# Loading a kernel's first batch in long runs: rotary embedding and scores on one core

## The chip, the cores and the metric

The kernel runs on one core of one Trainium2 chip. The metric is the device time of one execution in microseconds (us). The same kernel varies by some 0.2% from run to run.

## The reference

```python
batch, seq, heads, dim = 16, 512, 16, 64          # q, k: [batch, seq, heads, dim], float32
q_rot = np.concatenate([q1 * cos_q - q2 * sin_q, q1 * sin_q + q2 * cos_q], axis=-1)
k_rot = np.concatenate([k1 * cos_q - k2 * sin_q, k1 * sin_q + k2 * cos_q], axis=-1)
scores = np.einsum('bshd,bthd->bsht', q_rot, k_rot)   # [16, 512, 16, 512], float32
```

67 MB are read and 268 MB are written, against little arithmetic.

## The kernel before

A partition holds four neighbouring positions of a batch, the "slots" `c = 0..3`. A batch of q or of k is then 16 KB of unbroken memory per partition. VectorE rotates, TensorE transposes and multiplies, ScalarE copies the scores to a stage buffer of 4 MB, and SyncE asks for all large transfers on one queue. There are three stage buffers; the third holds the first batch of q and k at the start.

The first batch is treated apart: its unit of work is not a slot but a group of four heads over all four slots, so that the compute can start when these heads have landed. Its loads follow that grouping:

```python
    def load_units(which, head, heads):                 # runs of heads*64*4 bytes
        ...
        src = dram[which][0, :, :, head : head + heads, :]
        nc.sync.dma_start(t.rearrange("p c (h d) -> p c h d", d=D), src)
        for h in range(0, heads, G):
            units[which, (head + h) // G] = t[:, :, D * h : D * (h + G)]
...
        for head, heads in ((0, G), (G, H - G)):        # G = 4: 1 KB runs, then 3 KB runs
            load_units("k", head, heads)
            load_units("q", head, heads)
        load("k", 1)
        load("q", 1)
...
        for which in ("k", "q"):
            run(rope(which, 0))                          # rotate heads 0..3 of all four slots
            tr_act(which, 0)
        for i in range(C):                               # first batch; its stores are 1 MB each
            ...
            for p in range(HP):
                scores(i, p, st)
                ...
                if p == 3 and i < 2:
                    load("kq"[i], 2)                     # third batch of k, of q
        load("k", 3)
        for i in range(C, NST):                          # steady part; a 4 MB store each
            ...
```

## Time and profile before

| | before |
|---|---|
| median of 3 runs | 799.22 us (799.08 to 800.84) |
| span of the profiled run | 798.6 us |
| bytes moved | 336.17 MB |
| busy: PE, DVE, ACT | 690, 545, 561 us |
| share of q1 in the 16 DMA engines' span | 98.7% |

A busy TensorE at 86% might look like the bound; but the DMA engines are busy all the time, so only their idle time and the length of their packets count. The lines are shown in the prediction.

### The profile page before, as it was taken

The page shows a single profiled execution, that of the slowest core. Times are in us where ns is not written, and L with a number is a line of the kernel's source. Part 1 is how long each engine was busy: PE and PEld are TensorE (multiplying, and loading weights), DVE is VectorE, ACT ScalarE, POOL GpSimd, SP SyncE. Part 2 cuts the span into 40 slices and gives each one's busy share as a digit, 9 for nine tenths or more (in the row PEclk, how much of TensorE's full clock was granted, in tenths as well). Part 3 has the DMA queues.
Part 4 walks back from the last instruction along what each step waited for, and adds up shares of the span by engine and source line. Part 5 has one row for each costly group of instructions (what it writes and reads, how often), then busy time and mean ns, then how long its engine had stood idle before and what let it go on. Part 6 is the DMA issues. An engine that isn't in the chain of part 4 may idle for free.

```text
span 798.6 us, 7719 instructions
## 1 busy us (share of the span) xinstructions
PE 690.1 (86%) x3072; PEld 299.2 (37%) x3072; DVE 544.5 (68%) x516; ACT 561.3 (70%) x647; POOL 0.7 (0%) x6
## 2 busy tenths in 40 slices
PE   4999998997979789797897988979889798899970
PEld 2444443433434334343343433424334243344420
DVE  7999987676857568575685766857758577586300
ACT  3888886776848668485785866858668586688770
POOL 0000000000000000000000000000000000000000
PEclk9999999899989899898998998999989899899995
DMA  9999999999999999999999999999999999999995
GB/s 357 421 411 435 437 423 433 423 427 440 421 431 429 429 437 427 436 421 434 426 432 434 431 420 429 434 429 437 427 424 407 443 422 440 423 404 419 426 426 235
DMA packets 17988, 336.17 MB, mean 421 GB/s; under 512 B 1824, under 2 KB 3104, under 8 KB 4384
## 3 DMA queue, kind: packets, MB, share of 16 engines
q1 hardware_dynamic: 17664, 335.55, 98.7%
q8 instruction: 24, 0.39, 0.2%
q10 hardware_dynamic: 288, 0.13, 0.1%
q14 instruction: 12, 0.10, 0.0%
HBM read 67.24 MB, written 268.44 MB: 420 GB/s over the span
## 4 chain that ended last, share of the span: by engine, by line
DMA 51%; PE 38%; ACT 4%; DVE 3%; issue 1%; ACTq 0%; SPq 0%
DMA out_dram<-st 48%; PE ps L166 29%; PE bank L127 9%; ACT st L173 4%; DMA q_sb<-in_q_dram 2%; DVE part L106 1%; DMA sin_t<-in_sin_dram 0%; DVE q_sb L107 0%; DVE k_sb L111 0%; DVE k_sb L107 0%; DVE q_sb L111 0%; DVE early L107 0%; DVE kT_t L142 0%; ACTq L281 0%; DVE early L111 0%
## 5 line engine op out<-in xcount | busy, mean ns | idle before, releaser
L173 ACT COPY st<-ps 128x1024 f32<-128x1024 f32 x512 | 495.0, 1019 | 203.4 <-DMA out_dram<-st 112.3
L166 PE MATMUL ps<-kT_t,qT_t 64*128 64x512 f32 x2048 | 547.9, 653 | 72.1 <-ACT st L173 72.1
L166 PEld LDWEIGHTS ps<-kT_t,qT_t 64*128 64x128 f32 x2048 | 185.0, 197 | 261.9 <-issue 140.6
L142 DVE COPY qT_t<-bank 128x512 f32<-128x512 f32 x118 | 81.5, 691 | 203.8 <-PE bank L127 203.8
L127 PEld LDWEIGHTS bank<-ident,q_sb 128*128 128x128 f32 x480 | 55.5, 151 | 102.4 <-issue 99.8
L127 PE MATMUL bank<-ident,q_sb 128*128 128x128 f32 x480 | 86.7, 308 | 0.9 <-PE ps L166 0.9
L127 PEld LDWEIGHTS bank<-ident,k_sb 128*128 128x128 f32 x480 | 50.5, 141 | 95.0 <-DVE k_sb L107 37.5
L127 PE MATMUL bank<-ident,k_sb 128*128 128x128 f32 x480 | 78.7, 287 | 1.2 <-DVE qT_t L142 1.2
L142 ACT COPY kT_t<-bank 128x512 f32<-128x512 f32 x122 | 72.5, 599 | 6.2 <-PE bank L127 6.2
L107 DVE TENSOR_TENSOR q_sb<-q_sb,cos_t 128x1024 f32<-128x1024 f32 x60 | 73.5, 1225 | 2.1
L111 DVE TENSOR_TENSOR k_sb<-k_sb,part 128x1024 f32<-128x1024 f32 x60 | 73.5, 1225 | 2.1
L107 DVE TENSOR_TENSOR k_sb<-k_sb,cos_t 128x1024 f32<-128x1024 f32 x60 | 73.5, 1225 | 2.0
L106 DVE TENSOR_TENSOR part<-q_sb,ss_t 128x1024 f32<-128x1024 f32 x60 | 73.5, 1225 | 2.0
L106 DVE TENSOR_TENSOR part<-k_sb,ss_t 128x1024 f32<-128x1024 f32 x60 | 73.0, 1216 | 0.1
L111 DVE TENSOR_TENSOR q_sb<-q_sb,part 128x1024 f32<-128x1024 f32 x60 | 72.9, 1216 | 0.0
L127 PE MATMUL bank<-ident,early 128*128 128x128 f32 x64 | 10.5, 316 | 12.3 <-DVE early L111 10.4
L127 PEld LDWEIGHTS bank<-ident,early 128*128 128x128 f32 x64 | 8.3, 161 | 17.3 <-issue 13.2
L106 DVE TENSOR_TENSOR part<-early,ss_t 128x1024 f32<-128x1024 f32 x8 | 9.8, 1223 | 5.7 <-ACT ss_t L198 5.5
L111 DVE TENSOR_TENSOR early<-early,part 128x512 f32<-128x512 f32 x16 | 10.3, 687 | 0.2
L107 DVE TENSOR_TENSOR early<-early,cos_t 128x1024 f32<-128x1024 f32 x8 | 9.8, 1225 | 0.3
L142 ACT COPY qT_t<-bank 128x512 f32<-128x512 f32 x10 | 5.7, 630 | 3.2 <-PE bank L127 3.2
L142 DVE COPY kT_t<-bank 128x512 f32<-128x512 f32 x6 | 4.1, 684 | 0.0
(9 smaller groups left out, 2.8 us busy)
## 6 DMA issues: line engine op xcount, KB each, us to landing
out_dram<-st SPq DMA_DIRECT2D x58, 4096.0 KB, 24.1
k_sb<-in_k_dram SPq DMA_DIRECT2D x15, 2048.0 KB, 27.6
q_sb<-in_q_dram SPq DMA_DIRECT2D x15, 2048.0 KB, 27.6
out_dram<-st SPq DMA_DIRECT2D x16, 1024.0 KB, 13.7
out_dram<-st SPq DMA_DIRECT2D x1, 3584.0 KB, 22.8
out_dram<-st SPq DMA_DIRECT2D x1, 3328.0 KB
early<-in_k_dram SPq DMA_DIRECT2D x1, 1536.0 KB, 8.8
early<-in_q_dram SPq DMA_DIRECT2D x1, 1536.0 KB, 12.0
```

What stands on the lines that cost most here:

```text
L106: nc.vector.tensor_tensor(pv, xs, ss, op=mult)
L107: nc.vector.tensor_tensor(xc, xc, cs, op=mult)
L111: nc.vector.tensor_tensor(y, y, z, op=add)
L127: nc.tensor.transpose(bank[:, x, :], src, ident)
L142: copy(out=dst, in_=src)
L166: nc.tensor.matmul(out=po, lhsT=lhs[64 * r : 64 * r + 64, :], rhs=rh, start=True, stop=True)
L173: nc.scalar.copy(out=so, in_=si)
```

## The change

It means to make the first 4 MB faster (long runs in place of 1 KB and 3 KB ones) and to keep the queue filled until the first store by asking for the third k early.

```diff
-    def load_units(which, head, heads):
-        ...
+    first = {}
+    for x, which in enumerate("kq"):
+        t = early[:, C * H * D * x : C * H * D * (x + 1)]
+        first[which] = t.rearrange("p (c e) -> p c e", c=C)
+    units = {(w, n): first[w][:, :, G * D * n : G * D * (n + 1)] for w in "kq" for n in range(C)}
 ...
     def load(which, b):
 ...
+        for x, y in ((0, 1), (1, 2), (2, C)) if (which, b) == ("k", 0) else ((0, C),):
+            nc.sync.dma_start(
+                t[:, x:y].rearrange("p c (h d) -> p c h d", h=H), dram[which][b][:, x:y]
+            )
 ...
-        for t, src in ((cos_t, cos), (sin_t, sin)):
+        for t, src in ((sin_t, sin), (cos_t, cos)):
 ...
-        for head, heads in ((0, G), (G, H - G)):
-            load_units("k", head, heads)
-            load_units("q", head, heads)
-        load("k", 1)
-        load("q", 1)
+        for which, b in (("k", 0), ("q", 0), ("k", 1), ("q", 1), ("k", 2)):
+            load(which, b)
 ...
-                if p == 3 and i < 2:
-                    load("kq"[i], 2)
+                if p == 3 and i == 1:
+                    load("q", 2)
```

The unit of compute stays a group of heads over all slots. It now needs all pieces of a batch.

More of the change, by code (lines that the diff above doesn't have):

```diff
@@ L58 @@
     early = stage_pool.tile([P, 2 * C * H * D], fp32, tag="stage", name="early")
-    units = {}
-    used = [0]
-    def load_units(which, head, heads):
-        n = C * heads * D
-        t = early[:, used[0] : used[0] + n].rearrange("p (c e) -> p c e", c=C)
-        used[0] += n
-        src = dram[which][0, :, :, head : head + heads, :]
-        nc.sync.dma_start(t.rearrange("p c (h d) -> p c h d", d=D), src)
-        for h in range(0, heads, G):
-            units[which, (head + h) // G] = t[:, :, D * h : D * (h + G)]
+    first = {}
[3 more added lines that the diff above has]
+    units = {(w, n): first[w][:, :, G * D * n : G * D * (n + 1)] for w in "kq" for n in range(C)}
     batches = {}
@@ L76, in load @@
             return
-        t = in_pool.tile([P, C, H * D], fp32, tag=which + "_in", name=which + "_sb")
-        batches[which, b] = t
-        nc.sync.dma_start(t.rearrange("p c (h d) -> p c h d", h=H), dram[which][b])
+        if b == 0:
+            t = first[which]
+        else:
+            t = in_pool.tile([P, C, H * D], fp32, tag=which + "_in", name=which + "_sb")
+            batches[which, b] = t
+        for x, y in ((0, 1), (1, 2), (2, C)) if (which, b) == ("k", 0) else ((0, C),):
+            nc.sync.dma_start(
+                t[:, x:y].rearrange("p c (h d) -> p c h d", h=H), dram[which][b][:, x:y]
+            )
     def rope(which, n):
```

## The prediction

> **What bounds the kernel now.** I read the page's head and slices first, then its DMA queues, then the stretches of the start and of the end, then SyncE's issues in order of time, and last VectorE's first instructions.
>
> ```profile
> span 798.6 us, 7719 instructions
> ...
> DVE  7999987676857568575685766857758577586300
> ...
> DMA  9999999999999999999999999999999999999995
> GB/s 357 421 411 435 437 423 433 423 427 440 421 431 429 429 437 427 436 421 434 426 432 434 431 420 429 434 429 437 427 424 407 443 422 440 423 404 419 426 426 235
> ...
> q1 hardware_dynamic: 17664, 335.55, 98.7%
> ```
>
> The DMA row is full in 39 of 40 slices, and SyncE's queue q1 alone fills 98.7% of the 16 engines' span. So the kernel takes what 336 MB take, plus whatever time the DMA engines stand still. Only two places have such time: the start and the tail.
>
> ```profile
> 2.00:4.00 2.00, 0.00 (x0) 0.00 (x0) 0.00 (x0) 0.91 (x1) 0.00 (x0) 1.00 0.87 239
> 6.00:10.00 4.00, 0.58 (x3) 0.61 (x4) 3.90 (x5) 0.00 (x0) 0.00 (x0) 1.00 1.01 390
> 13.00:23.00 10.00, 9.73 (x44) 5.32 (x44) 9.72 (x11) 7.03 (x10) 0.00 (x0) 1.00 1.03 437
> 73.00:83.00 10.00, 10.00 (x52) 4.42 (x50) 9.83 (x10) 8.67 (x11) 0.00 (x0) 1.00 1.05 451
> 83.00:93.00 10.00, 10.00 (x52) 4.42 (x50) 9.59 (x10) 8.67 (x11) 0.00 (x0) 1.00 0.99 424
> 93.00:103.00 10.00, 10.00 (x52) 4.41 (x50) 8.53 (x9) 8.67 (x11) 0.00 (x0) 1.00 1.00 433
> ```
>
> The columns are the stretch, its length, busy time of PE, PEld, DVE, ACT and POOL, the granted clock, the DMA share and GB/s. From 6 to 10 us the engines are busy (1.01) and still move only 390 GB/s: those are the 3 KB packets of the first batch. At 13 us the 16 KB packets begin, and 437 GB/s go through. In the last three lines TensorE has no idle time at all, so a delay of the compute is not made up there; note that these slots take 10 us each.
>
> ```profile
> 0.73 0.66 SPq L67 DMA_DIRECT2D early<-in_k_dram  x1
> ...
> 2.77 0.63 SPq L67 DMA_DIRECT2D early<-in_q_dram  x1
> ...
> 4.18 0.65 SPq L79 DMA_DIRECT2D q_sb<-in_q_dram  x1
> ...
> 19.09 3.23 SPq L176 DMA_DIRECT2D out_dram<-st  x2
> 22.37 0.71 SPq L79 DMA_DIRECT2D k_sb<-in_k_dram  x1
> ```
>
> ```profile
> 62.28 0.62 SPq L79 DMA_DIRECT2D k_sb<-in_k_dram  x1
> 73.25 20.37 SPq L147 DMA_DIRECT2D out_dram<-st  x3
> ```
>
> Loads are asked for by 4.2 us and fill the queue until 23.3 us (worked out below); the first store comes at 19.09. In the second fence, three stores of 4 MB (from 73.25 to 93.6 us) come with no load between them: the thinnest place of the queue after the first stores.
>
> ```profile
> 5.51 1.23 DVE L106 TENSOR_TENSOR part<-early,ss_t 128x1024 f32<-128x1024 f32 x1 [5.51 <-ACT ss_t L198]
> ...
> 9.36 1.22 DVE L106 TENSOR_TENSOR part<-early,ss_t 128x1024 f32<-128x1024 f32 x1
> ```
>
> VectorE begins the rotation of k's first four heads at 5.51, when the sine table is ready (the data had landed), and goes straight on to q's at 9.36. From then to 73 us it is busy 9.7 to 9.8 of each 10 us, so a late start stays late.
>
> **What the Trainium skill says.** "DMA: Bandwidth & Descriptors", section "Why small descriptors are slow (HBM only)", gives each packet a fixed overhead. The trace agrees: by its packet records 1 KB takes 46.8 ns, 3 KB 125, 8 KB 310, 16 KB 614, 32 KB 1215.5 ns, that is 350, 393, 423, 427 and 431 GB/s over 16 engines. The same page, "Where 436 GB/s comes from", puts the ceiling at 435; the 431 of the large stores lies just under it, so packet size has little left to give outside the start. Its section "Latency and other measured facts" gives 600 ns to the first byte of a transfer from SyncE; here the first issue at 0.73 is followed by the first packet at 2.18 us, 1.45, more than twice that, and the trace decides. "Anatomy of one DMA" says that completion, not setup, makes most of the fixed cost; the first batch's large k and q transfers landed at 10.9 and 14.8, about 1.4 us after I put their last packets.
>
> **The change part by part.** It leaves the instructions of VectorE, TensorE and ScalarE, their order and their sizes as they are (the two builds agree there but for two access patterns with one more dimension). What moves is the queue.
>
> *Packets of the first batch.* Each transfer is spread over 16 engines, so 128 partitions give 8 packets per run and engine. Before: 32 x 46.8 ns = 1.50 us twice (0.5 MB each in 1 KB) and 32 x 125 = 4.00 twice (1.5 MB each in 3 KB), 11.00 us. With the tables' packets the queue begins at 2.45 and the batch ends at 13.45; the trace has the first 16 KB packet at 13.37. After: two slots of k in 4 KB (no packet of 4 KB exists before; from the slope between 8 and 16 KB, 0.037 ns per byte and 6 ns fixed, I estimate 158 ns, so 8 x 158 = 1.26 us each), two more in 8 KB (8 x 310 = 2.48), q in 16 KB (8 x 614 = 4.91). k is through at 7.45 and q at 12.37. This saves 1.08 us of queue time, if the queue is then never empty.
>
> *The first compute comes later.* This is the hidden part. The first rotation takes heads 0 to 3 of all four slots. Before, that was one transfer of 0.5 MB; now these heads are scattered over all three pieces of k, and q's over 2 MB. So k is ready at 7.45 + 1.4 = 8.85 (rotated by 12.7 at 3.8 us), and q at 12.37 + 1.4 = 13.77. VectorE's second rotation starts at 13.8 in place of 9.36: a delay of 4.4 us. VectorE's fullness up to 73 us and TensorE's from 73 to 103 leave nothing to absorb it, so every store issue up to there moves by 4.4. Taking the 4 KB pieces of k gains nothing for the first rotation, which needs them all; the sine table ahead of the cosine gains nothing either, as k is now the later one.
>
> *The third k ahead of the first store.* The loads in the queue now last until 12.37 + 3 x 4.91 = 27.1. The first store, at 19.09 + 4.4, can start 1.35 us later (my estimate of issue to first packet, a little under the 1.45 of the first load), at 24.8. No gap there. Without this part there would be one of 2.6 us (loads until 22.2).
>
> *The thin place.* I let the queue serve transfers in order. Before: loads to 23.27, then 16 stores of 1 MB (8 x 310 = 2.48 each) and three loads (4.91 each) to 77.7; the trace has the first packet of the first 4 MB store at 77.76, so the bookkeeping holds. That store could have started at 73.25 + 1.35 = 74.6, a lead of 3.1 us. A 4 MB store takes 8 x 1215.5 = 9.72, less than the 10.02 between store issues, so the lead of the next is 2.8 and of the third 2.5. Then the load at 93.72 comes behind and the lead grows past 7. After: the queue is through at 27.1 + 39.68 + 9.82 = 76.6, and the store can start only at 73.25 + 4.4 + 1.35 = 79.0. The engines stand still for 2.4 us, then 0.3 before each of the next two: 3.0 in all.
>
> *Sum.* -1.08 (packets) + 2.99 (gaps) = +1.9 us; put shortly, 4.4 of delay less the smallest lead of 2.5. Everything from 113 us on waits for the queue, which has no idle time to the tail, so this stays to the end: 799.2 + 1.9 = 801.1 us.
>
> **The rivals.** First, the intended outcome: faster packets and no gap, 799.2 - 1.1 = 798.1. For it speaks that the place the change visibly guards, the first store, is covered. Against it stand the leads of 3.1, 2.8 and 2.5 us, which a delay of over 3.6 (2.5 plus the 1.1 gained) eats up. Second, the compute makes up part of its delay: ScalarE waits 3.0 us for a stage buffer at 37.5 to 40.5 us, a wait that falls away because the first stores no longer stand behind the third k. If that wait set the pace, the shift at 73 us would be 1.4 and the result again 798.1. Against it: VectorE never paused in that stretch, so it was not waiting for ScalarE. Third, a larger delay: 4 KB reads slower than estimated, or a landing lag that grows with a full queue. At 5.5 us of delay the cost is 3.0, so 802.2. Fourth, a wait of the start that the steady part hides: unlikely, as a part that is bound by the queue has no slack to hide idle time of the queue.
>
> **Range and chances.** My sum gives 801.1, its rivals 798.1 and 802.2, and the three times before spread over 1.8 us by themselves. Leaning to my own sum with some weight on the faster rivals, I predict 801.0 with 798.2 to 803.0. A move of 2% is 16 us, over five times any of these: 0.5% for faster, 98.5% for within, 1% for slower.
>
> **What would show it.** The first packets of 16 KB should end near 12.4 us, the second rotation start near 13.8, the first store issue at 23.5 and the first 4 MB store at 77.6. The DMA share should fall below 1 between 76 and 79 us (about 2.4 us lost) and nowhere else from 6 us on to the tail. If the second rotation starts at 13.8 but the 4 MB store is issued before 76, the compute caught up and my second rival is right; if that store is at 77.6 and the DMA share stays full, my bookkeeping of the queue is wrong. If the rotation starts before 12, the delay is mis-sized.

## The result, and the profile after

The changed kernel takes 802.94 us (median of 6, 801.68 to 803.26) against 800.49 (799.08 to 804.19) for the kernel before in the same rounds. The ratio is 1.0023, with a 95% interval of 1.0000 to 1.0046. Ratios here are the mean time of one kernel's runs over that of the other's of the same rounds, so not quite the ratio of the medians quoted. 0.0023 of 800 us is 1.8 us. On another occasion the ratio was 1.0033 (1.0019 to 1.0046), so a small loss is clear of the noise.

The page of the changed kernel, the same rows as before:

```profile
span 801.3 us, 7716 instructions
...
DVE  4999988586867668657686676857758577586300
...
DMA  9999999999999999999999999999999999999996
GB/s 368 423 394 395 418 392 437 427 431 430 431 424 429 425 433 429 432 427 437 429 428 433 434 427 433 427 438 429 431 428 434 427 429 408 429 429 393 419 441 252
...
q1 hardware_dynamic: 16128, 335.55, 98.5%
```

The 40 slices of 20 us are too coarse: the DMA row still reads 9 everywhere. Only the first numbers tell something: 368 for 357 in the first slice is the gain, and 394, 395, 418, 392 for 411, 435, 437, 423 in the third to the sixth are the loss. Finer stretches show where. First the kernel before (columns as in the prediction: the last two are the DMA share and GB/s), then the changed one:

```profile
78.00:80.00 2.00, 2.00 (x14) 0.78 (x10) 2.00 (x3) 1.93 (x3) 0.00 (x0) 1.00 1.00 426
...
88.00:90.00 2.00, 2.00 (x14) 0.80 (x10) 1.97 (x2) 1.91 (x3) 0.00 (x0) 1.00 0.95 410
...
98.00:100.00 2.00, 2.00 (x14) 0.82 (x10) 1.97 (x2) 1.89 (x3) 0.00 (x0) 1.00 1.03 442
```

```profile
74.00:78.00 4.00, 3.16 (x16) 1.63 (x18) 3.97 (x6) 2.72 (x4) 0.00 (x0) 1.00 1.03 430
78.00:80.00 2.00, 2.00 (x11) 0.67 (x8) 1.97 (x2) 1.77 (x3) 0.00 (x0) 1.00 0.27 115
80.00:88.00 8.00, 8.00 (x40) 3.76 (x42) 7.86 (x9) 6.82 (x9) 0.00 (x0) 1.00 1.07 459
88.00:90.00 2.00, 2.00 (x11) 0.65 (x8) 1.93 (x3) 1.85 (x3) 0.00 (x0) 1.00 0.63 262
90.00:98.00 8.00, 8.00 (x40) 3.78 (x42) 7.67 (x8) 6.82 (x9) 0.00 (x0) 1.00 1.07 457
98.00:100.00 2.00, 2.00 (x11) 0.64 (x7) 1.96 (x2) 1.85 (x3) 0.00 (x0) 1.00 0.61 262
```

From 78 to 80 us the DMA engines are 27% busy, and there are smaller dips ahead of the next two stores. (The shares over 1 beside the dips show that a packet is counted whole in one stretch, so the dips at 88 and 98 look deeper than they are; from the packets' starts and ends the idle time is 1.36 us at 79 and 0.47 us at 90 and 100 together.) TensorE and VectorE are busy all the while: it is the data for the store that is late. SyncE's issues show how late:

```profile
24.76 14.60 SPq L176 DMA_DIRECT2D out_dram<-st  x6
39.41 0.42 SPq L77 DMA_DIRECT2D q_sb<-in_q_dram  x1
...
79.35 20.37 SPq L147 DMA_DIRECT2D out_dram<-st  x3
```

The first store is issued at 24.76 (before: 19.09), and the first 4 MB store at 79.35 (before: 73.25). The delay is 5.7 us at the start and 6.1 us at the thin place, in this pair of traces. VectorE shows the cause:

```profile
9.24 1.23 DVE L106 TENSOR_TENSOR part<-early,ss_t 128x1024 f32<-128x1024 f32 x1 [9.24 <-DMA early<-in_k_dram]
...
14.11 1.23 DVE L106 TENSOR_TENSOR part<-early,ss_t 128x1024 f32<-128x1024 f32 x1 [1.05 <-DMA early<-in_q_dram]
```

Both first rotations now wait for data, the first for the whole k, the second for the whole q: at 14.11 in place of 9.36, so 4.75 us later. The remaining 1.3 us of this pair come from TensorE. Its first twelve score matmuls, before and after:

```profile
15.14 3.66 PE L166 MATMUL ps<-kT_t,qT_t 64*128 64x512 f32 x12
```

```profile
19.89 5.07 PE L166 MATMUL ps<-kT_t,qT_t 64*128 64x512 f32 x12
```

The page "TensorE: Matmul & The Clock Gate" of the Trainium skill, section "What's actually happening", says that TensorE runs at half its clock until it has been busy for a window of about 3.4 us, and falls back after an idle one. The traces agree: in the changed kernel pairs of these matmuls start 853 ns apart while slow and 430 ns apart later. The column PEclk of the stretches reads 1.00 throughout, because the trace has no clock record so early; its first record, of the full clock, begins at 16.83 us before and at 24.40 after, just where the matmuls become fast. Two of the twelve are slow (over 1 us long) before, and ten after.

It would be wrong to call this an effect of the change. Both kernels were traced a second time (runs f2_before_again and f1_after_again below), and then the kernel before had eight slow ones and the changed kernel six. Their twelve matmuls and their first 4 MB stores, first the kernel before, then the changed one:

```profile
15.74 4.66 PE L166 MATMUL ps<-kT_t,qT_t 64*128 64x512 f32 x12
...
74.78 20.37 SPq L147 DMA_DIRECT2D out_dram<-st  x3
```

```profile
19.88 4.39 PE L166 MATMUL ps<-kT_t,qT_t 64*128 64x512 f32 x12
...
78.67 20.37 SPq L147 DMA_DIRECT2D out_dram<-st  x3
```

In this second pair the delay at the thin place is 3.9 us (78.67 for 74.78), and at the second rotation 4.1 us (14.10 for 9.96). So the wait for the data makes a delay of 4 to 5 us, and the slow start of TensorE, which differs from run to run in both kernels, adds to it or takes from it.

### The profile page after: what moved, and what is told of

Read it like the earlier page. It is cut to its first block, busy times and chain, and to the rows that moved or that the text cites. A ratio compares the mean times of both kernels' runs of the same rounds, so it can differ in the third digit from the quotient of the medians.

```text
span 801.3 us, 7716 instructions
## 1 busy us (share of the span) xinstructions
PE 686.1 (86%) x3072; PEld 297.6 (37%) x3072; DVE 544.5 (68%) x516; ACT 561.8 (70%) x647; POOL 0.7 (0%) x6
## 4 chain that ended last, share of the span: by engine, by line
DMA 48%; PE 38%; DVE 5%; ACT 5%; issue 1%; ACTq 0%; SPq 0%; DVEq 0%
DMA out_dram<-st 47%; PE ps L166 29%; PE bank L127 9%; ACT st L173 5%; DVE part L106 2%; DMA early<-in_k_dram 1%; DVE early L111 1%; DVE k_sb L107 1%; DVE k_sb L111 1%; DVE early L107 1%; DVE kT_t L142 0%; DVE q_sb L107 0%; DVE q_sb L111 0%; ACTq L278 0%; SPq L77 0%
```

## The experiments

The theory: the late start of the compute carries through to about 110 us, as VectorE and then TensorE are busy nearly all the time up to there; where the queue's lead over the stores is smaller than the delay, the DMA engines stand still, and that time is lost for good. Its rivals: the loss is in the packets of the new loads; it is in the early third k; or it is chance. Kernels are compared only within the same rounds.

### One half of the change alone

```diff
 # kernel before, plus only the early third k
         load("q", 1)
+        load("k", 2)
 ...
-                if p == 3 and i < 2:
-                    load("kq"[i], 2)
+                if p == 3 and i == 1:
+                    load("q", 2)
```

> The kernel before with only the third k asked for ahead of the first store; the first batch still comes by heads. Theory (the loss is idle time of the DMA queue at the three 4 MB stores from 79 us on, made by the late start of the compute): the compute starts as before, so there is no gap; ratio 1.000, and under 0.1 us of DMA idle time between 74 and 104 us. Rival (moving the third k forward is itself the loss, as it holds back the first stores): ratio about 1.002.

Measured: 1.0004 (0.9989 to 1.0018), with 0.06 us of idle time between 15 and 110 us. The early third k alone is harmless.

```diff
 # changed kernel, the third k where it was before
-        for which, b in (("k", 0), ("q", 0), ("k", 1), ("q", 1), ("k", 2)):
+        for which, b in (("k", 0), ("q", 0), ("k", 1), ("q", 1)):
 ...
-                if p == 3 and i == 1:
-                    load("q", 2)
+                if p == 3 and i < 2:
+                    load("kq"[i], 2)
```

> The changed kernel, but the third k asked for where the kernel before asks for it. Theory: the loads run out near 22.7 us and the first store can be moved at about 25.6, so the queue stands still for about 3 us there and near 1 us ahead of the second store; being later, it then has no gap at 79 us. In all about 4 us idle, 2 more than the changed kernel: ratio about 1.005. Rival (the loss comes from the third k being early): ratio 1.000 or below.

Measured: 1.0063 (1.0049 to 1.0077), 5 us more than before. The gap has moved, as expected, from 79 us to the first store, and none is left at 79. The stretches of this run:

```profile
20.00:23.00 3.00, 3.00 (x11) 1.47 (x12) 2.93 (x4) 1.52 (x3) 0.00 (x0) 1.00 0.91 388
23.00:26.00 3.00, 3.00 (x18) 1.55 (x16) 2.90 (x5) 2.97 (x6) 0.00 (x0) 1.00 0.42 175
```

The idle time is 2.4 us, less than the 4 expected, yet the time lost is 5. So there is a second cost beside the idle time. The packet records show it: in the load of the third k, which follows the gap, 16 KB packets take up to 1.5 us in place of 611 ns, and that load and the stores around it lose 1.7 us. I come back to this below.

### More delay

```diff
 # changed kernel, first q behind the second k
-        for which, b in (("k", 0), ("q", 0), ("k", 1), ("q", 1), ("k", 2)):
+        for which, b in (("k", 0), ("k", 1), ("q", 0), ("q", 1), ("k", 2)):
```

> The changed kernel with the first q asked for behind the second k, so that q lands 4.9 us later and nothing else changes. Theory: every store up to 110 us moves by 4.9 more and the gap grows by as much: about 6.7 us of idle time before the third 4 MB store, ratio about 1.0085. Rival (the late start is hidden, the loss is elsewhere): 1.0023 as the changed kernel.

Measured: 1.0093 (1.0078 to 1.0108), 7.4 us over the kernel before. The second rotation starts at 19.05, 4.9 us later than in the changed kernel, and the loss grows by 5 to 6 us. It was not foreseen that most of the new gap opens at the first stores, before 79 us:

```profile
28.00:32.00 4.00, 4.00 (x24) 2.02 (x22) 3.89 (x5) 3.96 (x6) 0.00 (x0) 1.00 0.57 236
82.00:84.00 2.00, 2.00 (x13) 0.77 (x10) 1.93 (x3) 1.92 (x3) 0.00 (x0) 1.00 0.56 238
```

In all 5.1 us are idle between 15 and 110 us (expected 6.7).

### Delay without the change

The next two alter only the order of the four loads of the kernel before: the same packets, the same bytes, the third k in its old place.

```diff
 # kernel before; first experiment
-        for head, heads in ((0, G), (G, H - G)):
-            load_units("k", head, heads)
-            load_units("q", head, heads)
+        load_units("k", 0, G)
+        load_units("k", G, H - G)
+        load_units("q", 0, G)
+        load_units("q", G, H - G)
 # second experiment: the last two lines in the other order
```

> The kernel before with its first four loads in another order: k's 4 heads, k's 12 heads, q's 4 heads, q's 12 heads. Packets and bytes as before; q's first heads land near 10.9 instead of under 9. Theory: the second rotation starts about 1.5 us later, less than the smallest lead of the queue, 2.5 to 3.0 us, so no gap and a ratio of 1.000 for a delay of 1.5 to 2.9 us. Rival (every us of late start costs a us): 1.002 to 1.003.

> The kernel before with its first four loads in the order k's 4 heads, k's 12, q's 12, q's 4. Packets and bytes as before, so no packet is faster or larger. Theory: q's first heads land near 14.9, the second rotation starts 5.5 us later, with cold matmuls all stores near 79 us move by about 6.8, and the gap is 6.8 - 3.0 = 3.8 us (2.5 without the cold matmuls): ratio 1.003 to 1.005. Rival (the loss of the changed kernel comes from its larger packets or from the early third k, neither of which is here): 1.000.

The second, measured: 1.0063 (1.0047 to 1.0079), 5 us. The second rotation starts at 14.97, the first store is issued at 24.73 (as in the changed kernel), and the queue stands still:

```profile
23.00:26.00 3.00, 3.00 (x20) 1.60 (x18) 2.93 (x4) 3.00 (x5) 0.00 (x0) 1.00 0.38 158
```

Neither the long runs nor the early third k are in this kernel, and it loses as much as the changed kernel without its guard, and more than the 1.003 to 1.005 expected. So the late start alone makes such a loss. I had put the gap at 79 us; without the early third k it must come at the first store (issued at 24.7, loads through at about 23.3), and it does: 2.3 us idle.

The first, measured: 1.0017 (1.0004 to 1.0030), where 1.000 was expected. Here the theory was too simple. The second rotation starts 1.9 us late, the first store is issued at 21.78, the engines never stand still (0.16 us in all from 15 to 110 us), and still some 1.3 us are lost. The trace has 1.3 us of slow packets in the third k's load and around it, near 30 us: the second cost again, this time behind a queue that was only thin.

### Taking the causes away

```diff
 # changed kernel, the stores of slots 4 to 6 as two halves
+        elif b == 1 and i < C + 3:
+            if p in (3, HP - 1):
+                h = 0 if p == 3 else H // 2
+                nc.sync.dma_start(o_v[b, i % C][:, h : h + H // 2], st[:, h : h + H // 2])
         elif b > 0 and p == HP - 1:
             store(i, st)
```

> The changed kernel, but the three 4 MB stores of the slots 4 to 6 (the thin place) go as two halves of 2 MB, the first as soon as its heads are done, about 5 us earlier. Theory: the gaps of 1.4, 0.2 and 0.2 us go away while the late start of the compute (about 6 us) stays; ratio 0.9990 to 1.0005, about 2 us below the changed kernel. Rival (the loss is in the packets of the first batch or of loads that collide with stores): it stays at 1.0023.

Measured: 1.0023 (1.0009 to 1.0037), which looks like the rival. Yet the gaps were gone (0.05 us idle from 75 to 110 us). It was 0.002 slower than expected. It ran beside the kernel before, not beside the changed kernel, so I repeated both (below).

```diff
 # changed kernel, TensorE kept busy while it waits
+    def keep_warm(n):
+        bank = ps_t_pool.tile([P, 4, P], fp32, tag="ps_t", name="bank")
+        for x in range(n):
+            nc.tensor.transpose(bank[:, x % 4, :], ident, ident)
 ...
             run(rope(which, 0))
+            keep_warm(80 if which == "k" else 30)
```

> The changed kernel with 80 and 30 dummy transposes of the identity on TensorE while it waits for the first rotated k and q; they go to a bank that nobody reads. Theory: the first score matmuls then take 590 ns each instead of 1054, the first store is issued about 1.4 us earlier (23.4 instead of 24.8), and the gap at 79 us shrinks by about 1.3 us: ratio about 1.0007. Rival (the slow matmuls are of the first ones whatever came before): no change of either.

Measured: 1.0022 (1.0010 to 1.0034). The mechanism is as expected: the twelve matmuls and the stores are

```profile
19.39 2.85 PE L166 MATMUL ps<-kT_t,qT_t 64*128 64x512 f32 x12 [0.24 <-ACT qT_t L142]
```

```profile
22.52 15.05 SPq L176 DMA_DIRECT2D out_dram<-st  x6
...
78.06 20.37 SPq L147 DMA_DIRECT2D out_dram<-st  x3
```

so 2.85 us in place of 5.07 and 4.39, the first store 2.2 and 2.0 us earlier than in the two traces of the changed kernel, and the one at the thin place 1.3 and 0.6 us earlier. (The dummy transposes begin at 1.35 us, and the clock record at 4.32.) But the gap did not shrink (1.89 us), and the time did not fall: the expected 1.0007 was missed. In this run the load of q at 42 us had no slow packets (0.1 us), so the queue, too, reached the thin place earlier. In the changed kernel the slow packets there (0.9 to 1.5 us) had kept the queue busy for about as long as the slow TensorE held back the store.

Four kernels beside each other on one chip:

> The changed kernel unchanged, so that the variants beside it are compared on one chip, and so that its gaps and its slow loads are seen in a second trace. Theory (idle gaps at the 4 MB stores, plus slow packets in the loads that come soon after the queue ran thin): ratio 1.002 to 1.004 over the kernel before, gaps of 1.5 to 2 us between 75 and 105 us again, and again 2 to 3 us of excess over the usual 611 ns in the load packets near 45 and 112 us. Rival (the slow packets are chance): they lie elsewhere or are below 1 us in all.

> The kernel before against itself: the ratio should be 1.000 within about 0.001, which shows what a difference of 0.2% is worth here. Its trace should again have no gap before the tail, and under 1.5 us of slow load packets in the first 130 us.

> The changed kernel with the stores of slots 4 to 6 as halves, now beside the changed kernel. If the gaps cost what they last, it is 1.5 to 2 us below the changed kernel (0.002), with a rest of 0.5 to 1.5 us over the kernel before from slow loads near 45 us. If the gaps cost nothing (they are made up by other idle time later), it is level with the changed kernel, as the first run of it against the kernel before suggested.

> Both mends at once: halves and the dummy transposes that keep TensorE warm. Theory: the queue is neither empty nor thin at 45 or 80 us, so no gaps and no slow loads remain and the 0.5 us gained by the packets of the first batch shows: ratio 0.9990 to 1.0002, the best of all. Rival (the gaps cost nothing, and the loss has a cause not yet named): 1.002, level with the changed kernel.

| kernel | median, us | ratio to before (95%) |
|---|---|---|
| before, against itself | 800.10 | 1.0004 (0.9992 to 1.0017) |
| changed | 802.40 | 1.0033 (1.0019 to 1.0046) |
| changed, stores in halves | 801.63 | 1.0021 (1.0006 to 1.0035) |
| changed, halves and warm TensorE | 800.97 | 1.0011 (0.9997 to 1.0026) |

Each mend takes off about 0.001. The steps between neighbours lie within the intervals, so the timed runs alone do not show that the gaps cost what they last; from the changed kernel to the last row the difference is 0.0022, or 1.8 us. No version beats the kernel before: the best one comes level with it at most.

The traces are clearer when one asks at what time a given number of bytes had gone through the queue. At 60 MB (145 us) the two traces of the changed kernel are 3.9 and 3.4 us behind the mean of the two traces of the kernel before (which lie 0.3 us to either side of it); the two with halves are 0.4 us behind and 0.6 us ahead, and the one with both mends is 0.4 us ahead. So without the gaps the early loss is gone, although the compute is as late.

The stretch of the first gap in the version with halves:

```profile
78.00:80.00 2.00, 2.00 (x12) 0.91 (x10) 1.97 (x2) 1.91 (x3) 0.00 (x0) 1.00 1.04 442
```

and the stretches of the fourth q's load, near 110 us, in the repeated changed kernel, and then in the version with both mends:

```profile
106.00:113.00 7.00, 7.00 (x36) 3.33 (x38) 5.60 (x6) 6.27 (x7) 0.00 (x0) 1.00 0.94 342
113.00:117.00 4.00, 4.00 (x22) 1.75 (x20) 3.90 (x5) 3.36 (x5) 0.00 (x0) 1.00 1.00 328
```

```profile
106.00:113.00 7.00, 7.00 (x34) 3.15 (x36) 5.60 (x7) 5.75 (x8) 0.00 (x0) 1.00 1.07 452
113.00:117.00 4.00, 4.00 (x22) 1.79 (x20) 3.90 (x4) 3.82 (x5) 0.00 (x0) 1.00 0.98 422
```

From 113 to 117 us the engines are fully busy in both, and move 328 GB/s in one and 422 in the other: packets in flight that take longer. Idle time is not the only way for a queue to lose. The next table is from the packet records: idle time of the 16 engines, and by how much packets took longer than the median of their size (611 ns for 16 KB, 1213 for 32 KB, 309 for 8 KB), in us averaged over the 16 engines.

| run | idle 15 to 110 us | slow packets 20 to 60 us | slow packets 100 to 120 us |
|---|---|---|---|
| before | 0.05 | 1.06 | 0.24 |
| before, repeated | 0.07 | 0.47 | 0.87 |
| early third k alone | 0.06 | 0.30 | 0.32 |
| changed | 1.95 | 1.73 | 2.12 |
| changed, repeated | 2.00 | 1.12 | 2.03 |
| warm | 1.95 | 0.53 | 2.03 |
| first q behind second k | 5.07 | 2.42 | 1.98 |
| long runs alone | 2.42 | 2.35 | 1.34 |
| before, q's first heads third | 0.16 | 1.56 | 0.41 |
| before, q's first heads fourth | 2.32 | 2.21 | 0.75 |
| halves, two runs | 0.17, 0.12 | 1.75, 0.68 | 0.26, 0.19 |
| halves and warm | 0.07 | 0.62 | 0.15 |

All four runs with a gap at 79 us have 2 us of slow packets from 100 to 120 us: 1.2 to 1.3 us in the next load, the fourth q's, and the rest in the stores beside it. The three with the gap filled have a quarter of a us, though their compute is as late. But a gap just before is not needed: the long runs alone have 1.3 us there without one, and the repeated kernel before 0.9. What goes with the slow packets in these records is how shortly before its turn a load was asked for (numbers of the 13 traces, the load's own packets alone):

| load | issued before its first packet, us | lost by its packets, us |
|---|---|---|
| third k | 3.4 to 3.7 (3 traces) | 1.1 to 1.4 |
| third k | 4.2 or more (10) | 0.0 to 0.3 |
| third q | 3.4 to 3.7 (4) | 0.7 to 1.3 |
| third q | 4.4 or more (9) | 0.0 to 0.4, once 0.7 |
| fourth k | 4.8 or more (13) | 0.0 to 0.5 |
| fourth q, behind a 4 MB store | 10.7 to 10.9 (5) | 1.0 to 1.3 |
| fourth q, behind a 4 MB store | 11.1 to 11.5 (2) | 0.6 to 0.7 |
| fourth q, behind a 4 MB store | 11.7 to 13.1 (3) | 0.2 to 0.3 |
| fourth q, behind halves | 8.5 to 8.8 (3) | 0.1 to 0.2 |

So a queue that is only thin pays too, as the experiment with q's first heads third had shown. Why, no run here shows: nothing was varied to test it.

## Why the prediction was right

The result, 802.94 us and a ratio of 1.0023, lies in the range, and the predicted difference of 1.9 us is close to what was measured (1.8, and 2.6 later). That it is so close is luck: at 145 us the kernel was 3.4 to 3.9 us behind, twice the sum, and the rest of the run gave about half of that back. The mechanism stands: the first rotation needs all slots, so the compute starts late; up to the thin place nothing makes it up; the place that pays is the three 4 MB stores with no load between them, not the first store that the change guards. The gaps lie where they were put, and the order of sizes was right (one large, two small). Several terms were off, and they cancelled:

- *The delay* at the thin place was 6.1 us in the first pair of traces and 3.9 in the second, against 4.4. The landing of q gave 4.75 and 4.1. What is left over is the moment at which TensorE becomes fast; the prediction did not have it, and it differs from run to run. The first 4 MB store, put at 77.6, was issued at 79.35 and 78.67.
- *From issue to first packet* I took 1.35 us. On an empty queue the 4 MB store, issued at 79.35, has its first packet at 80.18: 0.83 us. So every lead was 0.5 us larger than computed.
- *The gaps* were put at 3.0 us in all and came to 1.95 and 2.0. With the first pair's delay of 6.1 and 0.83 us to start, the same sum would give more (6.1 + 0.5 gained by the packets - 2.5 of lead - 0.5 of the start = 3.6 us); slow packets near 45 us, which kept the queue busy longer, make up part of the difference.
- *The packets of the first batch* were to save 1.08 us. From the cumulated bytes the changed kernel is 0.54 us ahead at 16 us (about 0.75 in the second pair of traces). The 4 KB packets are part of the reason: their median is 159 ns, as estimated, but in the first two transfers, where the queue starts, they lose 0.6 to 0.7 us against it. (The prediction says that no 4 KB packet exists before; there are 128 in the last stores, also at 159 ns. And its 46.8 ns for 1 KB is near the median, 46; the mean is 51.5.)
- *Slow packets*, about 2 us near 112 us, were not in the sum at all.
- *The tail* gave some back: the idle time from 600 us on was 8.3 and 8.9 us in two traces of the kernel before, and 7.9 and 7.7 in two of the changed one. I do not know why. So "this stays to the end" was not borne out: of 4.0 and 3.7 us at 564 us, the spans have 2.65 and 1.45 left.

From the two traces of each, in us: idle 15 to 110, +1.9; slow packets over the whole run (8.2, 7.3 against 9.9, 8.8), +1.6; the nominal time of the first batch's packets (10.7 against 9.9 by their medians), -0.8; idle from 600 us, -0.8. The sum, 1.9, meets the spans (798.6 and 798.7 against 801.3 and 800.1, +2.05).

Of the rivals, the compute did not make up its delay (ScalarE's wait for a stage buffer did fall away, and changed nothing), and the intended outcome failed for the reason given against it. What stays open is the remainder of the mended versions. The two traced runs of the version with halves are 0.75 us longer than those of the kernel before (799.7 and 799.1 against 798.6 and 798.7), and slow packets over the whole run account for it (+1.0 us); but all its timed runs together say 0.002, or 1.7 us. In bytes the two traces are still level at 564 us (0.7 us behind and 0.6 ahead) and fall behind by 0.4 and 1.1 us after it, where the change touches nothing. The other 1 us, of the runs without a trace, is not located.

## What to carry to other kernels

Where a queue bounds a kernel, the idle time that a later start makes is not the delay but the delay less the queue's smallest lead: work out that lead at every store or load of the first phase, not only at the first one. Before making transfers longer, ask which instruction waits for them; here long runs saved 0.5 to 0.8 us and made the first rotation wait for four times the bytes. When a bound queue runs thin or dry, look also at what it does next: here the packets of the next load and of the stores beside it lost about as much again as the gap.

## What the Trainium skill lacked or had wrong

- "DMA: Bandwidth & Descriptors", "Latency and other measured facts": about 600 ns to the first byte; here 0.83 us from the issue of a 4 MB store on an empty queue, and 1.45 us for the first load of a kernel with 1 KB runs.
- The same page, "Why small descriptors are slow (HBM only)": a cost per packet alone does not describe a load that is asked for shortly before its turn; 23 of the 128 16 KB packets of one took 1.0 to 1.9 us in place of 611 ns, and with the stores beside it 2 us were lost. None of the sections I used has it.
- "TensorE: Matmul & The Clock Gate": nothing wrong; slow matmuls at 853 ns a pair against 430 fit the half clock. How many of the first twelve were slow differed from run to run of one kernel: two and eight before, ten and six after.
